# One-layer streaming encoder on one core: tokens, per-layer inputs and cached keys arrive features first, and the gate splits its per-layer inputs itself

## The chip, the core and the metric

The kernel runs on one core of one Trainium2 chip. Times are device microseconds of one execution of the program. The engines of the core are named as in the profile: PE (TensorE matmuls, with its weight loads as PEld), DVE (VectorE), ACT (ScalarE), POOL (GpSimd) and SP (SyncE, which here issues every DMA). The work is fp32 throughout; there is no change of data types between the two kernels.

## The reference

One layer over 2048 prompt tokens and 32 sample tokens, model width 1024, feed-forward width 4096, per-layer input width 256:

```
qa, ka, va, qb, kb, vb = split_proj(rmsnorm(h, g_attn), w_in)     # w_in 1024 x 3072
oa = diff_attn(qa, ka, va, t5_table, lam)     # 4 heads, two 64-wide maps, 128-wide values, chunk-causal
ob = band_attn(qb, kb, vb, band_table)        # 8 heads of 64, own chunk of 64 and the 8 before
h  = h + concat(rmsnorm(oa, subln_g) * (1 - lam_init), rmsnorm(ob, out_norm_b)) @ w_out
h  = h + relu(rmsnorm(h, g_mlp) @ w_up)**2 @ w_down
h  = h + (p @ w_ple_proj) * sigmoid(h @ w_ple_gate)               # p: per-layer input, 256 wide
y  = rmsnorm(h, g_final)
```

The sample tokens attend to cached keys and values (128 past rows) as well. Outputs are y for prompt and samples and the new keys and values of both attention groups.

## The kernel before

**Arithmetic.** A matmul of fp32 accuracy is made of three in a rounded fp32 form (fp32r): each operand is split into a high part (a copy in fp32r, on ACT or DVE) and a low part (operand minus high part, on POOL or DVE), and `mm3` (L213 to L218) adds high by high, low by high and high by low in PSUM. Splits are made by `split` (L178 to L187): ACT's part is L181, POOL's are L166 and L176, DVE's is L187. Weights come from HBM in units of 512 KB through `wunit` (L189): a load into a buffer `wr`, then `wh` (ACT) and `wl` (POOL).

**Layout.** The tokens are cut into four blocks of 512 (the last has the 32 samples too, 544). Activations are held with features on the partitions: `aH` and `aL` are 128 partitions x 8 x 512, eight groups of 128 features. The inputs arrive with tokens as rows, so the kernel turns them on PE, by a matmul against the identity matrix (`ident`).

**Stages**, with their place in the profiled execution, in us:

- 0 to 70: `prep` of blocks 0 and 1, and the value projection of attention group A. `prep` (L360) goes by tiles of 128 tokens: it loads `x` (512 KB), squares it on ACT (the sum for the norm), turns it in eight 128x128 pieces into `xp` in PSUM (L380), makes of each piece `aH` on ACT times the gain `g_attn` (L385) and `aL` on DVE (L386), copies `xp` to `xt` on DVE (L389), and stores `xt` as `xT` (512 KB) for the later residual. The value projection `vtile` (L418) makes 16 groups of 24 matmuls (`vps`): for each of two halves of the value weights and each of eight token tiles. ACT brings a group out of PSUM as `vraw` (L434, a ring of two buffers); from it DVE makes the split `vhl` (also a ring of two), and two stores go out, `va_p` (the output, 128 KB) and `vSa` (256 KB).
- 70 to 187: the bias tables, and the query and key projection of group A for blocks 0 and 1 (`qps`, 512 wide), woven with `prep_p`, which loads the per-layer inputs, turns them (`ppt`, L907), splits them and stores the split as `pS`.
- 187 to 476: attention A for the first queries, woven with group B's projections of blocks 0 and 1 and with `prep` of blocks 2 and 3.
- To about 1000: the projections of blocks 2 and 3, the cached keys and values (`caches`, L536, which turns the cached keys, `ctp`, L546), attention B, and the output projection of blocks 0 and 1.
- 1000 to 2080: the two first MLPs with the rest of attention A between, and the gate of block 1.
- 2080 to the end: output projections, MLPs and gates of the other blocks. `gate` (L1323) loads the split per-layer inputs (`pT`, four loads of 256 KB from `pS`), splits the residual `h` (`hu`), projects both and applies the sigmoid (`sig`).

**What sets the order.** The program is written as generators that are woven step by step; a scheduler at build time then fixes the order of every engine's instructions by readiness and priority (`prep` of blocks 2 and 3 has a raised priority). Each engine works its list in order. All DMAs are issued from SP's list, in order, and each of them waits until the one eight places before it has landed, so that at most eight are in flight. A buffer ring gives a buffer to the next user only when all who read it, stores included, are done.

Of the kernel before, what the change touches and what calls it, by code (L numbers as in the profile page):

```python
# [20 lines left out]
P = 128  # L21
# [122 lines left out]
class Kern:  # L144
# [95 lines left out]
    def consts(self, cp):  # L240
# [13 lines left out]
        self.g_attn = cols("g_attn_s", a["g_attn"][0], 8)  # L254
        self.rcol = cp.tile([P, 17], F32, name="rcol")

    def gains(self, cp):
        nc, a = self.nc, self.a

        def cols(name, ap, k):  # L260
            t = cp.tile([P, k], F32, name=name)
            self.dma(t, ap.rearrange("(k p) -> p k", p=P))
            return t

        self.g_mlp = cols("g_mlp_s", a["g_mlp"][0], 8)
        self.g_b = cols("g_b_s", a["out_norm_b"][0], 4)
        self.g_sub = cols("g_sub_s", a["subln_g"][0], 1)
# [75 lines left out]
    def scratch(self):  # L343
        self.xT = self.dram([P, 8, T], F32, "xT")
# [7 lines left out]
        self.pS = self.dram([P, 2, 2, T], F32, "pS")  # L352
# [7 lines left out]
    def prep(self, b, acts, pp, mm, tag, first=None):  # L360
# [3 lines left out]
        for i, (c0, n) in enumerate(toks(b)):  # L364
            t0 = 512 * b + c0
            x = pp.tile([P, D], F32, tag="x", name="x")
            self.dma(x[:n], self.xsrc(t0, n))
            if first is not None:
                first()
                first = None  # L370
            xt = pp.tile([P, 8, P], F32, tag="xt", name="xt")
            st = pp.tile([P, 1], F32, tag="st", name="st")
            nc.scalar.activation(
                xt[:n].rearrange("p a b -> p (a b)"), x[:n], AF.Square, accum_out=st[:n]
            )
            for h in range(2):
                xp = mm.tile([P, 4, P], F32, tag=tag, name="xp")
                for k in range(4):
                    kk = 4 * h + k
                    nc.tensor.transpose(xp[:, k, :n], x[:n, kk * P : kk * P + P], self.ident[:n, :n])  # L380
                for k in range(4):
                    kk = 4 * h + k
                    g = self.g_attn[:, kk : kk + 1]
                    hi, lo = aH[:, kk, c0 : c0 + n], aL[:, kk, c0 : c0 + n]
                    nc.scalar.activation(hi, xp[:, k, :n], AF.Copy, scale=g)  # L385
                    nc.vector.scalar_tensor_tensor(  # L386
                        lo, xp[:, k, :n], g, hi.bitcast(F32), op0=ALU.mult, op1=ALU.subtract
                    )
                nc.vector.tensor_copy(xt[:, 4 * h : 4 * h + 4, :n], xp[:, :, :n])  # L389
# [500 lines left out]
    def prep_p(self, sg, wk, ps):  # L890
        nc, a = self.nc, self.a
        for b in range(4):
# [4 lines left out]
            if b == 3:  # L897
                self.dma(pn[:SS, 4], a["p_sample"][0, 0])
# [817 lines left out]
```

## Time and profile before

| | |
|---|---|
| median of 3 runs | 3105.26 us (3106.78, 3105.26, 3100.71) |
| profiled execution, its own time | 3106.68 us |
| its span | 3104.9 us |
| PE busy | 2990.2 us, 96% of the span, 17801 matmuls |
| DVE, ACT, POOL busy | 1826.0, 1776.4, 1852.7 us |
| HBM read, written | 421.97 MB, 117.75 MB, 174 GB/s over the span |
| DMA packets under 512 bytes | 38749 of 523279 |

In a row of a view by windows, behind the stretch in us stand its length, then the busy time of PE, PEld, DVE, ACT and POOL with the number of instructions, then the clock that was granted to PE (1.00 is the full one), the mean busy share of the DMA engines, and GB/s. In a row of the timeline stand the start in us, the length, the engine, the line, what is written from what, and how many in a row; in square brackets is the idle time before it and what ended it. In a row of groups the busy time and the mean ns of one stand behind the bar, and then the idle time before such instructions. A tile's row has duration minimum, median and maximum in ns, and the first and last start. Matmuls overlap in their pipeline, so what a matmul adds is read from the distance of two starts.

### The profile page before, as it was taken

The numbers are of one execution on the slowest core, as the hardware profiler recorded it, in microseconds if no ns is written. First come the engines' busy times: TensorE is split into PE (matmuls) and PEld (weight loads), VectorE is DVE, ScalarE is ACT, GpSimd is POOL, SyncE is SP. The second block draws the span as 40 slices with busy tenths as digits, with TensorE's granted clock in tenths as the row PEclk, the third lists the DMA queues.
The fourth block names the chain that finished last, engine by engine and source line by source line (L and its number), as shares of the span: only waits on it lengthen the run. The fifth ranks groups of instructions, "written<-read, shape, count | busy, mean of one in ns | idle before, by whom it ended". The sixth has DMA issues, their size and how long they took to land. (4 is left out here: it accounts for less than half of the span.)

```text
span 3104.9 us, 51763 instructions
## 1 busy us (share of the span) xinstructions
PE 2990.2 (96%) x17801; PEld 2637.0 (85%) x17801; DVE 1826.0 (59%) x4404; ACT 1776.4 (57%) x3434; POOL 1852.7 (60%) x2512
## 2 busy tenths in 40 slices
PE   8999989999899999999999999999899999999998
PEld 7788879899777888878888888878788887999998
DVE  6157565564565455456666656635667885576663
ACT  6256565765666666556556556554655555554545
POOL 2456746413446544556655555677878888767674
PEclk9999999999999999999999999999999999999999
DMA  9798776976877554555655454348434446333231
GB/s 283 258 263 247 224 218 187 280 221 186 247 230 226 159 155 136 154 157 167 196 152 140 124 145 139 123 150 260 155 116 130 146 158 226 118 109 102 90 117 57
DMA packets 523279, 539.19 MB, mean 174 GB/s; under 512 B 38749, under 2 KB 401569, under 8 KB 523017
## 3 DMA queue, kind: packets, MB, share of 16 engines
q1 hardware_dynamic: 523016, 535.89, 57.5%
q8 instruction: 141, 2.31, 0.3%
q14 instruction: 122, 0.99, 0.1%
HBM read 421.97 MB, written 117.75 MB: 174 GB/s over the span
## 5 line engine op out<-in xcount | busy, mean ns | idle before, releaser
L176 POOL TENSOR_TENSOR wl<-wr,wh 128x256 fp32r<-128x256 f32 x648 | 478.9, 771 | 317.8 <-ACT wh L181 277.9
L181 ACT ACTIVATE piece<-wr 128x512 fp32r<-128x512 f32 x406 | 245.4, 624 | 265.0 <-PE ups L217 111.2
L176 POOL TENSOR_TENSOR piece<-wr,piece 128x256 fp32r<-128x256 f32 x404 | 327.5, 836 | 104.6 <-ACT piece L181 85.7
L181 ACT ACTIVATE wh<-wr 128x1024 fp32r<-128x1024 f32 x228 | 240.4, 1055 | 188.1 <-PE ups L217 46.8
L166 POOL TENSOR_TENSOR wl<-wr,wh 128x256 fp32r<-128x256 f32 x264 | 201.9, 797 | 188.1 <-ACT wh L181 185.3
L216 PE MATMUL dps<-uh,piece 128*128 128x272 f32 (+1 forms) x768 | 246.3, 324 | 6.2 <-DVE h L1217 2.5
L166 POOL TENSOR_TENSOR piece<-wr,piece 128x256 fp32r<-128x256 f32 x280 | 235.1, 871 | 26.7 <-ACT piece L181 25.5
L218 PE MATMUL dps<-uh,piece 128*128 128x272 f32 (+1 forms) x768 | 246.9, 324 | 1.8 <-POOL piece L166 1.6
L217 PE MATMUL dps<-ul,piece 128*128 128x272 f32 (+1 forms) x768 | 247.3, 323 | 0.2 <-DVE ul L187 0.2
L216 PE MATMUL ups<-cs,piece 128*128 128x256 f32 (+1 forms) x864 | 245.8, 285 | 0.9 <-DVE r L1228 0.8
L217 PE MATMUL ups<-cs,piece 128*128 128x256 f32 (+1 forms) x864 | 245.7, 285 | 0.0
L218 PE MATMUL ups<-cs,piece 128*128 128x256 f32 (+1 forms) x864 | 245.5, 284 | 0.0
L216 PE MATMUL qps<-aH,wh 128*128 128x512 f32 (+1 forms) x640 | 227.9, 357 | 1.1 <-DVE ql L488 1.1
L217 PE MATMUL qps<-aL,wh 128*128 128x512 f32 (+1 forms) x640 | 228.0, 356 | 0.0
L218 PE MATMUL qps<-aH,wl 128*128 128x512 f32 (+1 forms) x640 | 227.6, 356 | 0.0
L1217 DVE TENSOR_TENSOR h<-h,dps 128x272 f32<-128x272 f32 (+1 forms) x384 | 188.9, 514 | 52.6 <-PE dps L218 51.7
L1169 DVE TENSOR_TENSOR h<-h,dps 128x512 f32<-128x512 f32 x256 | 173.3, 682 | 69.0 <-PE dps L218 67.4
L665 ACT ACTIVATE e<-e,nm 128x128 f32<-128x128 f32 (+16 forms) x136 | 157.2, 1156 | 94.9 <-DVE nm L663 92.9
L216 PE MATMUL dps<-uh,wh 128*128 128x512 f32 x512 | 207.0, 404 | 1.8 <-DVE h L1169 1.8
L216 PE MATMUL ups<-cH,wh 128*128 128x512 f32 x512 | 202.8, 397 | 1.9 <-ACT cH L181 1.9
L217 PE MATMUL ups<-cL,wh 128*128 128x512 f32 x512 | 202.5, 396 | 1.8 <-POOL cL L166 1.2
L218 PE MATMUL ups<-cH,wl 128*128 128x512 f32 x512 | 202.7, 396 | 0.0
(311 smaller groups left out, 9369.8 us busy)
## 6 DMA issues: line engine op xcount, KB each, us to landing
wr<-w_up SPq DMA_DIRECT2D x128, 512.0 KB, 4.0
wr<-w_down SPq DMA_DIRECT2D x128, 512.0 KB, 3.9
wr<-w_in SPq DMA_DIRECT2D x74, 512.0 KB, 5.5
q<-qS SPq DMA_DIRECT2D x128, 256.0 KB, 5.2
v<-vSa SPq DMA_DIRECT2D x64, 512.0 KB, 4.8
ka<-kS SPq DMA_DIRECT2D x32, 512.0 KB, 6.8
wr<-w_out SPq DMA_DIRECT2D x32, 512.0 KB, 4.6
wr<-w_ple_gate SPq DMA_DIRECT2D x32, 512.0 KB, 4.2
```

Source lines behind the costliest of these rows:

```text
L166: nc.gpsimd.tensor_tensor(out[:, sl], a[:, sl], b[:, sl], op=op)
L176: nc.gpsimd.tensor_tensor(out[:, sl], a[:, sl], b[:, sl], op=op)
L181: nc.scalar.activation(hi, raw, AF.Copy)
L216: nc.tensor.matmul(ps, lh, rh, start=start and i == 0, stop=False)
L217: nc.tensor.matmul(ps, lh, rl, start=False, stop=False)
L218: nc.tensor.matmul(ps, ll, rh, start=False, stop=stop and i == n - 1)
L665: nc.scalar.activation(row, row, AF.Exp, bias=nmx, accum_out=z[:nr, m : m + 1])
L1169: nc.vector.tensor_tensor(hv, hv, ps, op=ALU.add)
L1217: nc.vector.tensor_tensor(hv, hv, ps, op=ALU.add)
```

## The change

The host hands over three arrays that it has laid out with numpy: `x_t` (128 x 8 x 2080, the tokens with features first), `p_t` (128 x 2 x 2080, the per-layer inputs likewise) and `ck_t` (the cached keys of both groups, features first). The four gain vectors come as [128, k], so that a partition's values lie together.

`prep` loads, for each tile of 128 tokens, the tile of `x_t` (`xt`) and the rows `x`; DVE multiplies `xt` by the gain in place, ACT and DVE split it, and ACT squares `x` in place for the sum. Nothing is turned and `xT` is not stored, since `x_t` takes its place. `prep_p` and `pS` are gone; the query and key projection of group A is no longer woven with anything. A new function `ptile` loads two raw halves of the per-layer inputs (`praw`) for a gate and splits them there; block 0's is called ahead of the output projection of block 2. `caches` loads the cached keys features first. The value weights' raw loads of the first stage have four buffers of their own (`wr0`) beside the ring `wr`.

```diff
     def wunit(self, src, shape, hi_eng="act", lo_eng="pool", pool=None):
         nc = self.nc
-        raw = self.rawp.tile([P] + shape, F32, bufs=2, name="wr")
+        if pool is None:
+            raw = self.rawp.tile([P] + shape, F32, bufs=2, name="wr")
+        else:
+            raw = pool.tile([P] + shape, F32, tag="wr0", bufs=4, name="wr0")
...
-            self.dma(t, ap.rearrange("(k p) -> p k", p=P))
+            self.dma(t, ap)
...
-        self.xT = self.dram([P, 8, T], F32, "xT")
+        self.xT = self.a["x_t"]
+        self.pT = self.a["p_t"]
...
-            x = pp.tile([P, D], F32, tag="x", name="x")
-            self.dma(x[:n], self.xsrc(t0, n))
+            xt = pp.tile([P, 8, P], F32, tag="xt", name="xt")
+            self.dma(xt[:, :, :n], self.xT[:, :, t0 : t0 + n])
...
-            xt = pp.tile([P, 8, P], F32, tag="xt", name="xt")
+            x = pp.tile([P, D], F32, tag="x", name="x")
+            self.dma(x[:n], self.xsrc(t0, n))
+            m = 2 if b == 0 and i == 0 else 1
+            for k in range(0, 8, 8 // m):
+                ks = slice(k, k + 8 // m)
+                xg = xt[:, ks, :n]
+                g = self.g_attn[:, ks].unsqueeze(2).broadcast_to([P, 8 // m, n])
+                nc.vector.tensor_tensor(xg, xg, g, op=ALU.mult)
+                self.split(aH[:, ks, c0 : c0 + n], aL[:, ks, c0 : c0 + n], xg, "act", "dve")
             st = pp.tile([P, 1], F32, tag="st", name="st")
-            nc.scalar.activation(
-                xt[:n].rearrange("p a b -> p (a b)"), x[:n], AF.Square, accum_out=st[:n]
-            )
-            for h in range(2):
-                xp = mm.tile([P, 4, P], F32, tag=tag, name="xp")
-                for k in range(4):
-                    kk = 4 * h + k
-                    nc.tensor.transpose(xp[:, k, :n], x[:n, kk * P : kk * P + P], self.ident[:n, :n])
-                for k in range(4):
-                    kk = 4 * h + k
-                    g = self.g_attn[:, kk : kk + 1]
-                    hi, lo = aH[:, kk, c0 : c0 + n], aL[:, kk, c0 : c0 + n]
-                    nc.scalar.activation(hi, xp[:, k, :n], AF.Copy, scale=g)
-                    nc.vector.scalar_tensor_tensor(
-                        lo, xp[:, k, :n], g, hi.bitcast(F32), op0=ALU.mult, op1=ALU.subtract
-                    )
-                nc.vector.tensor_copy(xt[:, 4 * h : 4 * h + 4, :n], xp[:, :, :n])
-            self.dma(self.xT[:, :, t0 : t0 + n], xt[:, :, :n])
+            nc.scalar.activation(x[:n], x[:n], AF.Square, accum_out=st[:n])
...
-            kn = sg.tile([P, 512], F32, tag="kn", bufs=2, name="ckn")
-            self.dma(kn, ck)
-            tps = tp.tile([P, 4, P], F32, tag="mm", name="ctp")
-            for g in range(4):
-                nc.tensor.transpose(tps[:, g], kn[:, P * g : P * g + P], self.ident)
+            tf = sg.tile([P, BLK], F32, tag="kr", bufs=2, name="ckr")[:, :512]
+            self.dma(tf, ck)
...
-    def prep_p(self, sg, wk, ps):
...
+    def ptile(self, b, up, wk):
+        n, t0 = BN[b], 512 * b
+        pT = [[up.tile([P, BLK], F32R, tag="u", name="pT") for _ in range(2)] for _ in range(2)]
+        for k in range(2):
+            raw = (
+                up.tile([P, up.aw], F32, tag="u", name="praw") if wk is None
+                else wk.tile([P, BLK], F32, tag="tmp", bufs=self.nt, name="praw")
+            )[:, :n]
+            self.dma(raw, self.pT[:, k, t0 : t0 + n])
+            self.split(pT[0][k][:, :n], pT[1][k][:, :n], raw, "act", "dve")
+        return pT
+
-        for i in range(2):
-            for k in range(2):
-                self.dma(pT[i][k][:, :n], self.pS[:, i, k, t0 : t0 + n])
+        if pT is None:
+            pT = self.ptile(b, up, wk)
...
-                qk = self.proj(HALVES[0], 0, acts, sg, mm, Rings((ps_t, "tp")), vs=())
-                weave(qk, self.prep_p(sg, wk, ps_t), 2)
+                drain(self.proj(HALVES[0], 0, acts, sg, mm, Rings((ps_t, "tp")), vs=()))
...
+                pT = self.ptile(0, up, wk)
                 weave(self.outproj(2, wk, oa[2], md, acc[2]), self.oload(3, wk, act, oa), 1, 0, 2)
...
-            g = self.gate(0, h, up, None, md, wk, made[0])
+            g = self.gate(0, h, up, None, md, wk, made[0], pT)
```

Where the instructions then stand is fixed by the scheduler. SP's list in the first stage, around the first store of values (`va_p`), before; `wr` with 4x256 are value weights, with 8x128 query and key weights, and x_4486 is a tile of block 2:

```order
L157 DMA x_423<-x_prompt 128x1024
L157 DMA wr_1188<-w_in 128x8x128
L157 DMA wr_1380<-w_in 128x8x128
L157 DMA x_4486<-x_prompt 128x1024
L157 DMA wr_227<-w_in 128x4x256
L157 DMA x_536<-x_prompt 128x1024
L157 DMA wr_236<-w_in 128x4x256
L157 DMA xT_83<-xt_125 1024x1x128
L157 DMA va_p<-vraw_277 128x256
L157 DMA x_643<-x_prompt 128x1024
L157 DMA vSa_86<-vhl_279 128x512
L157 DMA xT_83<-xt_186 1024x1x128
```

And now, on the same engine, at the same store; ahead of these rows stand eight loads of xt and x for block 0 and four of value weights, and xt_4182 and x_4184 are block 2's first tile:

```order
L157 DMA wr_901<-w_in 128x8x128
L157 DMA wr_976<-w_in 128x8x128
L157 DMA wr_1061<-w_in 128x8x128
L157 DMA wr_1144<-w_in 128x8x128
L157 DMA xt_4182<-x_t 128x8x128
L157 DMA x_4184<-x_prompt 128x1024
L157 DMA x_439<-x_prompt 128x1024
L157 DMA xt_437<-x_t 128x8x128
L157 DMA va_p<-vraw_228 128x256
L157 DMA vSa_85<-vhl_230 128x512
L157 DMA x_521<-x_prompt 128x1024
L157 DMA xt_519<-x_t 128x8x128
```

The first store of values stood behind 13 transfers of 512 KB and now stands behind 20, of which four are query and key weights and two belong to block 2.

ACT's list in the first stage, where blocks 0 and 1 meet, before; `aH_107<-xp` are single 128x128 pieces of block 1:

```order
L385 ACTIVATE aH_107<-xp_541,g_attn_s_122 128x128
L434 ACTIVATE vraw_309<-vps_284,rcol_124 128x256
L434 ACTIVATE vraw_384<-vps_359,rcol_124 128x256
L373 ACTIVATE xt_538,st_539<-x_536 128x1024
L385 ACTIVATE aH_107<-xp_555,g_attn_s_122 128x128
L385 ACTIVATE aH_107<-xp_541,g_attn_s_122 128x128
```

And now; vraw_310 is the third use of the ring of two, so it follows the store `va_p<-vraw_228` above, aH_105 is block 1's, and rsv and rsy are steps of a tile's norm:

```order
L181 ACTIVATE wh_1063<-wr_1061 128x1024
L396 ACTIVATE rbt_107<-rp_431 128x512
L384 ACTIVATE x_4184,st_4189<-x_4184 128x1024
L226 ACTIVATE rsv_4191<-st_4189 128x1
L228 ACTIVATE rsy_4193<-rsv_4191 128x1
L384 ACTIVATE x_439,st_444<-x_439 128x1024
L229 ACTIVATE rsy_4193<-rsy_4193 128x1
L226 ACTIVATE rsv_446<-st_444 128x1
L228 ACTIVATE rsy_448<-rsv_446 128x1
L229 ACTIVATE rsy_448<-rsy_448 128x1
L428 ACTIVATE vraw_310<-vps_285,rcol_122 128x256
L181 ACTIVATE aH_105<-xt_437 128x8x128
```

ACT's many small pieces became one instruction per tile, and squares of later tiles, block 2's among them, stand ahead of the third `vraw`.

ACT's list at the gate of block 2, before; `hu` is the split of the residual, `piece` that of weights, `uh` that of the MLP's hidden layer, `sig` the first step of the sigmoid:

```order
L181 ACTIVATE uh<-r_29347 128x512
L181 ACTIVATE piece<-wr 128x512 x2
L181 ACTIVATE hu<-h 128x512
L181 ACTIVATE piece<-wr 128x512 x2
L181 ACTIVATE hu<-h 128x512 x7
L181 ACTIVATE piece<-wr 128x512 x3
L1362 ACTIVATE sig<-gps 128x512
```

And now:

```order
L181 ACTIVATE uh<-r_28816 128x512
L181 ACTIVATE piece<-wr 128x512 x2
L181 ACTIVATE pT<-praw 128x512 x2
L181 ACTIVATE hu<-h 128x512 x2
L181 ACTIVATE piece<-wr 128x512 x2
L181 ACTIVATE hu<-h 128x512 x6
L181 ACTIVATE piece<-wr 128x512 x5
L1334 ACTIVATE sig<-gps 128x512
```

The two splits of the per-layer inputs stand ahead of the first split of the residual.

More of the change, by code (lines that the diff above doesn't have):

```diff
@@ L1687, with columns @@
 }
+def columns(*parts):
+    t = np.concatenate(parts).T
+    return np.ascontiguousarray(t.reshape(-1, P, T).transpose(1, 0, 2))
 def kernel(**inputs):
     arrays = {k: np.ascontiguousarray(v) for k, v in inputs.items()}
-    for n in ("cache_a_k", "cache_a_v", "cache_b_k", "cache_b_v"):
+    for n in ("cache_a_v", "cache_b_v"):
         arrays[n] = arrays[n].reshape(PAST, 512)
+    ck = [arrays.pop(n).reshape(PAST, 4, P) for n in ("cache_a_k", "cache_b_k")]
+    arrays["ck_t"] = np.ascontiguousarray(np.stack(ck).transpose(0, 3, 2, 1)).reshape(2, P, 512)
+    arrays["x_t"] = columns(arrays["x_prompt"][0], arrays["x_sample"][0])
+    arrays["p_t"] = columns(arrays.pop("p_prompt")[0, 0], arrays.pop("p_sample")[0, 0])
+    for n in ("g_attn", "g_mlp", "out_norm_b", "subln_g"):
+        arrays[n] = np.ascontiguousarray(arrays[n].reshape(-1, P).T)
     arrays["onehot_a"], arrays["onehot_b"] = onehots()
```

43 lines of the change are left out of this document (7 added, 36 removed).

## The prediction

> **What bounds the kernel now.** I read the page's busy shares first, then the windows by stage, and then the rows of each tile that the change touches.
>
> ```profile
> PE 2990.2 (96%) x17801; PEld 2637.0 (85%) x17801; DVE 1826.0 (59%) x4404; ACT 1776.4 (57%) x3434; POOL 1852.7 (60%) x2512
> ```
> ```profile
> 0.00:25.00 25.00, 16.07 (x93) 14.27 (x94) 13.33 (x47) 17.82 (x52) 8.58 (x19) 1.00 0.94 277
> 25.00:50.00 25.00, 23.86 (x201) 23.26 (x201) 19.98 (x67) 21.59 (x65) 11.92 (x18) 1.00 1.07 334
> 50.00:70.00 20.00, 20.00 (x170) 19.91 (x169) 9.89 (x35) 6.77 (x19) 0.00 (x0) 1.00 0.67 225
> 70.00:187.00 117.00, 114.21 (x567) 91.66 (x566) 27.29 (x69) 33.38 (x60) 45.62 (x66) 1.00 0.82 257
> 187.00:476.00 289.00, 268.75 (x1591) 235.40 (x1590) 184.61 (x550) 179.25 (x413) 185.44 (x270) 0.97 0.80 235
> ```
>
> PE is busy 96% of the span, so work taken from PE shortens the program unless PE then waits. The exception is the first 50 us: the DMA share is 0.94 and 1.07 there, at 277 and then 334 GB/s. From 70 to 187 us PE idles 2.8 us in 117, and from 187 to 476 20 us in 289. There the granted clock also falls, to 0.97, after long gaps:
>
> ```profile
> 326.67 0.58 PE L723 MATMUL o<-pH,v 128*128 128x256 f32 x1 [3.39 <-ACT rsv L223]
> 398.68 1.01 PE L650 MATMUL s<-ka,q 128*128 128x384 f32 x2 [4.87 <-DVE e L657]
> ```
> ```profile
> 327.00:336.00 9.00, 9.00 (x38) 7.97 (x38) 3.70 (x9) 4.20 (x10) 6.78 (x10) 0.69 0.85 260
> ```
> ```profile
> 399.00:407.00 8.00, 8.00 (x46) 7.91 (x46) 6.60 (x21) 5.55 (x14) 3.74 (x5) 0.67 0.60 187
> ```
>
> A gap of 3.39 us is followed by 9 us at 0.69, which loses 9 x 0.31 = 2.8 us more, and one of 4.87 us by 8 us at 0.67, 2.6 us more. I price a gap above about 3 us at its length plus 2.7.
>
> **The price of a turn on PE.** The 136 `xp` and 34 `ppt` transposes and the 8 `ctp` go.
>
> ```profile
> L380 PE MATMUL xp<-ident,x 128*128 128x128 f32 (+1 forms) x136 | 21.5, 289 | 6.2 <-DMA x<-x_prompt 4.4 <-DVE kr L493 1.1 <-ACT vraw L434 0.5
> ```
> ```profile
> 391.80 0.60 PE L380 MATMUL xp<-ident,x 128*128 128x128 f32 x4
> 392.24 0.82 PE L709 MATMUL tpp<-ident,e 128*128 128x128 f32 x6
> ```
>
> Four of them push the next instruction back by 392.24 - 391.80 = 0.44 us, 0.11 each; the whole group is busy 21.5 us, 0.158 each. I take 0.12, near the start-to-start value, since the busy time counts overlap with neighbours.
>
> **First stage, 0 to 70 us: +5.9 us.** 64 of the `xp` are here, 64 x 0.12 = 7.7 us of PE. If PE alone set its end, that would be the gain. But the stores decide:
>
> ```profile
> L218 PE MATMUL vps<-wh,aL x128: 277/283/582, 10.1 to 69.3; 128*128 128x256 f32 x128
> ```
> ```profile
> 36.37 1.83 PE L380 MATMUL xp<-ident,x 128*128 128x128 f32 x12
> 39.20 0.39 PE L216 MATMUL vps<-wh,aH 128*128 128x256 f32 x1 [1.00 <-ACT vraw L434]
> 39.43 0.28 PE L217 MATMUL vps<-wl,aH 128*128 128x256 f32 x1
> 39.55 0.28 PE L218 MATMUL vps<-wh,aL 128*128 128x256 f32 x1
> ```
> ```profile
> 17.98 3.04 SPq L157 DMA_DIRECT2D va_p<-vraw  x1
> ```
>
> The 16 `vps` groups end at 69.3 + 0.3 = 69.6. A matmul of them follows the one before by 39.55 - 39.43 = 0.12 us; over a long stretch 0.117, so a group of 24 takes 2.81. A group can start only when one of three PSUM banks is free, and ACT frees a bank by writing `vraw`, a ring of two that waits for the store `va_p`. Already before, PE stood 1.00 us for that at 39.20. The first `va_p` was issued at 17.98, behind 13 transfers of 0.524 MB. In SP's new order it stands behind 20, 10.5 MB. The first 25 us moved 25 x 0.277 = 6.9 MB. So it lands at about 25 + (10.5 - 6.9) / 0.334 = 36 us, and until then ACT stands at the third `vraw`, with the splits of block 1's tiles queued behind it. The store that frees the 8th group's bank is the third `va_p`, with 16.0 MB of transfers ahead of it by the same count: 25 + (16.0 - 6.9) / 0.334 = 52.2 us. The other bound takes the best rate of a stretch that I found, some 410 GB/s from 2584 to 2591 us (this row has 40 slices of 1 us from 2580 on):
>
> ```profile
> GB/s 335 349 383 409 409 406 417 415 400 413 417 347 324 352 385 403 337 332 362 409 414 409 404 349 306 291 305 356 383 377 376 338 236 100 291 176 8 237 287 44
> ```
>
> At 0.41 it is 25 + 9.1 / 0.41 = 47.2. From there nine groups take 9 x 2.81 = 25.3 us, so the stage ends between 72.5 and 77.5, plus 0 to 2.7 for a half clock after one gap. I take 75.5, the middle, +5.9 against 69.6; the ends are -7.7 (stores in time) and +13.3 (below). DVE and ACT have less to do: a tile costs DVE 8 x 0.343 + 2 x 0.678 = 4.1 us now and 2 x 1.382 = 2.8 at most then, and ACT 8 x 0.365 = 2.9 now and 1.06 then, by these rows (the three-operand one stands for an fp32 pass of 128x1024 on DVE):
>
> ```profile
> L386 DVE SCALAR_TENSOR_TENSOR aL<-xp,g_attn_s,aH 128x128 fp32r<-128x128 f32 x128 | 42.3, 343 | 29.4 <-ACT aH L385 29.2
> L389 DVE COPY xt<-xp 128x512 f32<-128x512 f32 x32 | 21.7, 678 | 0.0
> L671 DVE SCALAR_TENSOR_TENSOR e<-e,c 128x1024 f32<-128x1024 f32 x40 | 55.1, 1382 | 8.1 <-ACT e L670 8.1
> ```
> ```profile
> L385 ACT ACTIVATE aH<-xp,g_attn_s 128x128 fp32r<-128x128 f32 (+1 forms) x136 | 45.8, 365 | 23.5 <-DVE aL L386 21.1 <-PE xp L380 1.7 <-PE qps L217 0.3
> L181 ACT ACTIVATE wh<-wr 128x1024 fp32r<-128x1024 f32 x228 | 240.4, 1055 | 188.1 <-PE ups L217 46.8 <-issue 32.1 <-PE qps L217 20.8
> ```
>
> The gains as [128, k] spare SP a stand of at most 2.00 us, the one at `g_b_s`; the first group waits for weights and splits anyway, so nothing (0 to -2):
>
> ```profile
> 4.79 2.00 SPq L157 DMA_DIRECT2D g_b_s<-out_norm_b  x1
> ```
>
> **Query and key stage, 70 to 187 us: -6.2 us.** The 34 `ppt` go, 34 x 0.12 = 4.1 us, and with them two PE waits in the ring of PSUM banks that `ppt` shares with `ktp`, 1.82 + 0.33 = 2.1:
>
> ```profile
> 105.22 0.66 PE L516 MATMUL ktp<-ident,kr 128*128 128x128 f32 x4 [1.82 <-ACT kn L518]
> 106.44 0.66 PE L907 MATMUL ppt<-ident,pn 128*128 128x128 f32 x4 [0.33 <-DVE ppl L911]
> ```
>
> The stage is PE-bound (114.21 of 117), so what goes comes out: bounds -4 and -8.
>
> **Blocks 2 and 3, 187 to 476 us: -8.6 - 1.6 - 2.0 us.** 72 `xp` go: 72 x 0.12 = 8.6 (7.9 to 11.4), and PE's waits before them, 1.1 for `kr` and 0.5 for `vraw` in the group's row above. The rest of the gaps belong to attention's chain through DVE and ACT. These two lose work, 72 x 0.365 = 26 us on ACT and 9 tiles x 1.3 = 12 us on DVE, but the scheduler has redrawn the order of this whole stretch. I give -2, with -8 (a third of the 20 us of gaps closes) and +10 (three more gaps of the kind priced above) as the ends. **Cached keys**: 8 transposes, -1.0.
>
> **The gates: +4.0 us.** ACT splits the per-layer inputs twice per gate (0.63 us each) ahead of the residual's first split, and is in order: `hu` and the sigmoid's steps queue behind it, POOL's low parts wait for ACT, and PE for these. At the gate of block 2:
>
> ```profile
> 2597.60 0.63 ACT L181 ACTIVATE hu<-h 128x512 fp32r<-128x512 f32 x1 [1.11 <-DVE h L1217]
> 2599.85 1.15 ACT L181 ACTIVATE piece<-wr 128x512 fp32r<-128x512 f32 x2 [1.62 <-DMA wr<-w_ple_gate]
> 2600.91 3.55 ACT L181 ACTIVATE hu<-h 128x512 fp32r<-128x512 f32 x6
> ```
> ```profile
> 2590.44 0.38 SPq L157 DMA_DIRECT2D wr<-w_ple_gate  x1
> 2601.52 5.01 SPq L157 DMA_DIRECT2D pT<-pS  x4
> ```
> ```profile
> cs<-cSt SPq DMA_DIRECT2D x8, 544.0 KB, 10.1
> ```
>
> `pT` was fetched at 2601.52, after `hu` had begun. Now `praw` must be there before 2597.60. It is issued about where the weights of 2590.44 are, behind transfers that take 10.1 us to land, so about 2601: 3.4 late, and two splits of 0.63 make 4.7. ACT idled 1.62 us there for the weights, which hides that much: +3 (0 to +7.7, the whole 5 plus 2.7 for a half clock). Gates 1 and 3 get 0.5 each, between nothing and 2 x 0.63. At block 0's gate, where `ptile` comes early, ACT has room, so 0:
>
> ```profile
> 2062.73 1.06 ACT L181 ACTIVATE wh<-wr 128x1024 fp32r<-128x1024 f32 x1 [4.24 <-PE gps L217]
> ```
>
> **The sum.** +5.9 - 6.2 - 8.6 - 1.6 - 2.0 - 1.0 + 4.0 = -9.5, from the span of 3104.9 to 3095.4. The profiled execution took 3106.68, 1.8 above its span, and the median of the runs is 1.4 below it; 3106.7 - 9.5 - 1.4 = 3096 us.
>
> **Rivals.** *The stores land in time*, 3082: SP's prefetch costs nothing and the first stage gives its 7.7 us too (13.6 less than my sum). For it: DVE and ACT are lighter there. Against it: PE already waited for `vraw` with seven transfers fewer ahead. *The first stage is set by DMA*, 3103: the 8th group starts at 52.2 and two gaps above 3 us come before it, 52.2 + 25.3 + 5.4 = 82.9, 13.3 over 69.6 and 7.4 over my sum. For it: the DMA share of 1.07. *Slower, 3115*: ACT stands at the first `praw` split. If that costs gates 1, 2 and 3 the whole of 5 + 2.7 = 7.7 us each, it is 23.1 instead of 4.0. It decides for slower once these stands exceed 4.0 + 15.5 = 19.5 us together. For it: at 2597.60 PE has nothing but this gate to do. Against it: ACT's idle time at gates 1 and 3.
>
> The Trainium skill, in "TensorE: Matmul & The Clock Gate", Part 1, has the clock halve after an idle window of about 3.4 us and come back after about 3.4 us of steady work. By that a gap costs an estimated 1.7 us beyond itself, and the second rival would come to 3101; the trace's 9 us at 0.69 after a gap of 3.39 speak for more, and I keep the measured price.
>
> **How the numbers follow.** My forecast, with its own range of 3085 to 3104, has a chance of 0.46; stores in time 0.15; DMA-set first stage 0.16; slower by the gates 0.23. A measurement of this kernel tells about 0.2%, 6.2 us, from no change: 3099 to 3111.5 is "the same". Of the forecast's 0.46, 0.10 lies above 3099. So faster is 0.36 + 0.15 = 0.51, the same 0.10 + 0.16 = 0.26, slower 0.23. The range is 3079 to 3116: it takes in the rivals' times, and leaves 2 in 10 for sums of ends on one side.
>
> **What would show it.** In the profile after: the last `vps` near 75 us, with PE gaps ended by `vraw` between 25 and 55 and `vraw` ended by `va_p`; if the last comes before 65, the first rival. The query and key stage about 6 us shorter, and no gap at `ktp`. From 187 to the end of attention A's first part, 8 to 12 us less. At the gates, ACT's splits of `praw` with the load as releaser: where these waits pass 5 us, the last rival. I am wrong if the redrawn stretch costs more than its +10, or if later stages, whose PE order is unchanged, move.

## The result, and the profile after

The changed kernel takes 3075.25 us (median of 4 runs, 3073.95 to 3077.8) against 3102.99 us for the kernel before beside it: a ratio of 0.991, 95% interval 0.9894 to 0.9926, some 28 us faster. A second set of runs gave 0.9927 (0.9905 to 0.9948). Forecast were 3096 us and a range of 3079 to 3116, so the direction was right and the size was not.

The page's busy times after, and the windows after, cut at four places that both programs pass: the last value matmul of the first stage, the first score of attention A, the first score of attention B, and the first matmul of the first MLP.

```profile
PE 2965.4 (96%) x17623; PEld 2617.9 (85%) x17623; DVE 1815.5 (59%) x4268; ACT 1760.9 (57%) x3314; POOL 1870.7 (61%) x2512
```
```profile
0.00:78.60 78.60, 56.63 (x393) 54.20 (x394) 44.99 (x106) 43.63 (x99) 27.24 (x36) 0.93 0.96 302
78.60:175.70 97.10, 96.05 (x424) 75.27 (x423) 16.67 (x40) 27.23 (x51) 40.98 (x59) 1.00 0.75 234
175.70:528.80 353.10, 346.63 (x2242) 313.25 (x2239) 209.86 (x556) 206.02 (x404) 255.98 (x353) 1.00 0.78 229
528.80:952.10 423.30, 399.58 (x2438) 353.75 (x2439) 240.23 (x809) 281.71 (x595) 165.91 (x260) 0.97 0.79 230
952.10:1989.00 1036.90, 1019.82 (x5222) 858.44 (x5220) 609.89 (x1572) 627.18 (x1055) 577.71 (x818) 1.00 0.53 152
1989.00:3074.70 1085.70, 1046.72 (x6913) 962.93 (x6912) 693.83 (x1189) 575.12 (x1114) 802.84 (x989) 0.99 0.42 137
```

The same cut of the kernel before, in its windows:

```profile
0.00:69.60 69.60, 59.53 (x457) 57.12 (x458) 42.92 (x145) 46.01 (x134) 20.50 (x35) 1.00 0.91 282
69.60:177.90 108.30, 105.55 (x495) 82.90 (x493) 21.90 (x41) 28.41 (x46) 45.58 (x66) 1.00 0.79 255
177.90:547.50 369.60, 346.85 (x2181) 309.88 (x2181) 222.28 (x656) 221.04 (x494) 231.69 (x337) 0.98 0.77 228
547.50:981.20 433.70, 410.89 (x2554) 366.91 (x2555) 239.34 (x815) 286.35 (x607) 173.77 (x271) 0.98 0.80 231
```

A stage's length less PE's busy time is PE's idle time there. The first stage grew by 9.0 us. The query and key stage shrank by 11.2. From the first score to the first MLP 803.3 us became 776.4, 26.9 less; 15.4 of it is idle time (22.8 + 22.8 before, 6.5 + 23.7 after), nearly all of it between the first scores of attention A and B. The MLPs with attention A between took 1.2 us more and the rest, with all four gates, 2.3 less (1088.0 before).

### The profile page after: what moved, and what is told of

Same layout as the page of the kernel before. It is cut to its first block, busy times and chain, and to the rows that moved or that the text cites. A ratio compares the mean times of both kernels' runs of the same rounds, so it can differ in the third digit from the quotient of the medians.

```text
span 3074.7 us, 51058 instructions
## 1 busy us (share of the span) xinstructions
PE 2965.4 (96%) x17623; PEld 2617.9 (85%) x17623; DVE 1815.5 (59%) x4268; ACT 1760.9 (57%) x3314; POOL 1870.7 (61%) x2512
## 5 line engine op out<-in xcount | busy, mean ns | idle before, releaser
L176 POOL TENSOR_TENSOR wl<-wr,wh 128x256 fp32r<-128x256 f32 x648 | 493.0, 793 | 276.1 <-ACT wh L181 243.9
L166 POOL TENSOR_TENSOR wl<-wr,wh 128x256 fp32r<-128x256 f32 x264 | 200.2, 790 | 203.2 <-ACT wh L181 185.6
L220 PE MATMUL dps<-ul,wh 128*128 128x512 f32 x512 | 201.8, 394 | 0.0
L221 PE MATMUL dps<-uh,wl 128*128 128x512 f32 x512 | 201.7, 394 | 0.0
```

What stands on the lines that cost most here:

```text
L166: nc.gpsimd.tensor_tensor(out[:, sl], a[:, sl], b[:, sl], op=op)
L176: nc.gpsimd.tensor_tensor(out[:, sl], a[:, sl], b[:, sl], op=op)
L220: nc.tensor.matmul(ps, lh, rl, start=False, stop=False)
L221: nc.tensor.matmul(ps, ll, rh, start=False, stop=stop and i == n - 1)
```

## The experiments

The ratio is always to the kernel before, run beside it (median about 3104 us), and the idle time is PE's between the first scores of attention A and B, from one profile. Two profiles of one program can differ by some us: the changed kernel's second had a span of 3081.3 against 3074.7, and 6.2 us of this lay between first score and first MLP; for the kernel before, this stretch was 6.9 us shorter in the second. So a difference of one profile counts from about 7 us on.

The idle time between the two scores is not all: some orders have less of it there and more behind it. So this table gives the stages in us, with the whole stretch from the first score to the first MLP and PE's idle time in it:

| kernel | first stage | query and key | first score to first MLP | PE idle in that |
|---|---|---|---|---|
| before, two profiles | 69.6, 70.0 | 108.3, 108.3 | 803.3, 796.4 | 45.6, 44.2 |
| changed, two profiles | 78.6, 79.8 | 97.1, 96.6 | 776.4, 782.6 | 30.2, 36.5 |
| token part alone | 84.0 | 114.9 | 771.4 | 32.9 |
| per-layer part alone | 70.0 | 99.3 | 795.7 | 40.7 |
| before, first redraw | 67.5 | 106.7 | 789.5 | 35.2 |
| before, third redraw | 69.4 | 103.6 | 797.0 | 40.7 |
| changed, turns in blocks 2 and 3 | 76.1 | 95.8 | 786.4 | 33.3 |
| changed, all turns | 65.1 | 96.0 | 786.0 | 34.2 |
| changed, all turns and their store | 73.9 | 95.9 | 785.7 | 32.5 |

### The two halves of the change

Token part alone (before, with `x_t`, the new `prep` as in the change, and the four weight buffers):

```diff
-        self.xT = self.dram([P, 8, T], F32, "xT")
+        self.xT = self.a["x_t"]
```

> The kernel before with the token part alone (x_t from the host, the new prep, the four raw weight buffers); per-layer inputs, cached keys and gains as before. If the per-layer part is worth what the prediction counted (query and key stage -6.2, cached keys -1.0, gates +4.0), this is about 3 us slower than the whole change, some 3078 us. If, as the two traces suggest, the gates cost nothing, it is 8 to 9 us slower, some 3084. Both theories of the attention stretch (187 to 476 us before: less small work on ACT and DVE, or the turns gone from PE's order and PSUM banks) expect the stretch's gain of 27 us between the first score and the first MLP to be here whole.

Measured: 1.0009 (0.9994 to 1.0023), no change. The last value matmul comes at 83.7 us, and PE's gap for `vraw` is longer than in the whole change:

```profile
39.15 0.58 PE L219 MATMUL vps<-wh,aH 128*128 128x256 f32 x1 [6.87 <-ACT vraw L428]
```

Per-layer part alone:

```diff
-                qk = self.proj(HALVES[0], 0, acts, sg, mm, Rings((ps_t, "tp")), vs=())
-                weave(qk, self.prep_p(sg, wk, ps_t), 2)
+                drain(self.proj(HALVES[0], 0, acts, sg, mm, Rings((ps_t, "tp")), vs=()))
...
+            pT = self.ptile(b, up, wk)
```

> The kernel before with the per-layer part alone (p_t from the host, no prep_p, the gates split). The prediction's terms: -6.2 in the query and key stage and +4.0 at the gates, some 3101 us. With gates that cost nothing: some 3096 us. A theory by which any redrawing of the order is worth ten or more us either way expects it to lie outside 3090 to 3106.

Measured: 0.9948 (0.9927 to 0.9968), 16 us faster, where the terms of the prediction gave 2. Its idle time is 13.7 us, with all 136 turns still there. The token part, which takes most work from PE, earned nothing alone, so what was expected of its time fell. What was expected of the stretch held: in its profile (3098.68 us, where the median is 3106.12) the stretch from first score to first MLP is 25 to 32 us shorter than before. The first stage, 14 us longer, and the query and key stage, 7 longer, eat most of this.

### Did turns and pieces hold PE up?

Pieces of 128x128 again in blocks 2 and 3, without turns; and turns without a reader, without pieces:

```diff
-                self.split(aH[:, ks, c0 : c0 + n], aL[:, ks, c0 : c0 + n], xg, "act", "dve")
+                for kk in range(8):
+                    self.split(aH[:, kk, c0 : c0 + n], aL[:, kk, c0 : c0 + n], xt[:, kk, :n], "act", "dve")
```

> The changed kernel, with the splits of blocks 2 and 3 made again in eight pieces of 128x128 per tile on ACT and DVE (from SBUF, no turns on PE): per tile ACT 8 x 0.365 = 2.9 us instead of 1.06. Theory W (the attention stretch became shorter since ACT and DVE, in order, have fewer small instructions between attention's steps): PE's gaps in that stretch come back, +12 to +16 us, some 3089. Theory P (it became shorter since the turns are gone from PE's order and from the PSUM banks that the projections use): no change beyond 3 us.

```diff
+                xp = mm.tile([P, 4, P], F32, tag=tag, name="xp")
+                for k in range(4):
+                    kk = 4 * h + k
+                    nc.tensor.transpose(xp[:, k, :n], x[:n, kk * P : kk * P + P], self.ident[:n, :n])
```

> The changed kernel, with the 72 turns of blocks 2 and 3 back on PE, into the same PSUM banks, and nobody reading them (work added that serves nothing). Theory W: PE's work alone, 72 x 0.12 = +8.6 us, some 3084. Theory P: the turns' waits for loads and banks come back too, +18 to +24 us, some 3096.

Measured: 0.9946 (0.9928 to 0.9965) with pieces, 6 to 11 us slower than the changed kernel by its two ratios, and 0.9976 (0.9959 to 0.9994) with turns, 15 to 20 slower. The profiles say less: spans of 3075.9 and 3083.0, idle times of 12.3 and 6.4 us. Neither brings the 22.8 back. But the two profiled executions took 3077.65 and 3084.81 us, where the medians are 3083.27 and 3097.34, so they do not show all that these kernels lose. Whole preparations as before in blocks 2 and 3 settle what the turns do there (`prep_old` is the `prep` of before without its store):

```diff
-lifted(self.prep(2, acts, pp, mm, "mm"))
+lifted(self.prep_old(2, acts, pp, mm, "mm"))
...
-lifted(self.prep(3, acts, pp, mm, "mm"))
+lifted(self.prep_old(3, acts, pp, mm, "mm"))
```

> The changed kernel, with blocks 2 and 3 prepared as before (turns on PE, small pieces on ACT and DVE from PSUM, the copy on DVE; only the store of the turned block stays out), all else changed. Theory T (turns and small pieces, coupled through PSUM, hold PE up in the attention stretch): 72 x 0.12 = 8.6 us and some 14 us of idle time come back, +20 us or more, idle 18 us or more between the first score and attention B. Theory L (the draw of the order did it): +8.6 us, +6 to +12 in all, idle 6 to 12 us.

Measured: 0.992 (0.9902 to 0.9939) beside 0.9927 for the changed kernel in the same set, so no dearer, where 6 us were the least expected, and 7.2 us idle. The windows of this kernel from first score to attention B, and from there to the first MLP:

```profile
171.90:514.20 342.30, 335.12 (x2163) 301.21 (x2161) 224.45 (x656) 220.37 (x494) 231.12 (x332) 1.00 0.76 225
514.20:958.30 444.10, 418.02 (x2614) 375.69 (x2615) 243.39 (x826) 291.42 (x616) 179.09 (x281) 0.97 0.81 232
```

All the turns, small pieces and copies of these blocks are in them, and in the first PE still waits a third of what it did before; over the whole stretch it waits 33.3 us, between the changed kernel's 30.2 and 36.5. So the turns and their small pieces are not what held PE up (theory T falls). Their own price is not refuted: the stretch is 4 to 10 us longer than in the changed kernel's two profiles, for 72 turns put at 8.6, and the first stage 2.5 to 3.7 us shorter. The changed kernel beside it:

> The changed kernel itself, beside the runs of the other kernels of this call, so that they have a common scale: the ratio to the kernel before that it had, 0.991, within its interval of 0.989 to 0.993. If the earlier ratio was an accident of one chip, it lies nearer to 1.

### Was it the order that the scheduler drew?

The kernel before again, and three redraws of it that keep all its work:

> The kernel before itself, for a second profile. If the 22.7 us of PE idle time between its first score and attention B's first (69.6, 177.9 and 547.5 us) belong to its order of instructions, they stand there again, 20 to 25 us, with the gaps of 3.39 and 4.87 us at the same matmuls. If they were an accident of one execution, some 10 us.

```diff
                 nc.vector.tensor_copy(xt[:, 4 * h : 4 * h + 4, :n], xp[:, :, :n])
             self.dma(self.xT[:, :, t0 : t0 + n], xt[:, :, :n])
+            if b > 1:
+                nc.scalar.activation(x[:n], x[:n], AF.Square, accum_out=st[:n])
```

> The kernel before, with all its work; only in blocks 2 and 3 the square for the norm is written behind the turns and in place, so that the scheduler draws the order from 187 us on anew. Theory L (the kernel before had an unlucky order there, 20 us of PE idle time between 178 and 514 us, and any redrawing gets rid of it): that idle time falls to 6 to 11 us and the kernel becomes 8 to 14 us faster than before. Theory T (turns and small pieces themselves hold PE up): still some 20 us idle, within 4 us of before.

```diff
-                weave(qk, self.prep_p(sg, wk, ps_t), 2)
+                drain(qk)
+                drain(self.prep_p(sg, wk, ps_t))
```

> The kernel before, with all its work; only the turning of the per-layer inputs is written behind the query and key projection instead of woven with it. Theory L: the order behind it is drawn anew, and the idle time between 178 and 514 us falls by about 10 us, 8 to 12 us faster than before (some 3092). Theory T: within 4 us of before.

```diff
-                weave(qk, self.prep_p(sg, wk, ps_t), 2)
+                weave(qk, self.prep_p(sg, wk, ps_t), 1)
```

> The kernel before, with the turning of the per-layer inputs woven after every step of the query and key projection instead of every second: no work added or taken, a large redraw. Theory L (the order before was an unlucky one): idle time between first score and attention B of 10 to 14 us, and 6 to 12 us faster than before. If the work that was removed had made the difference: some 20 us idle and within 4 us of before.

The kernel before repeats itself, at 1.0004, with 22.2 us idle and a gap at the same score:

```profile
398.47 1.01 PE L650 MATMUL s<-ka,q 128*128 128x384 f32 x2 [5.99 <-DVE e L657]
```

The three redraws, in the order above: 0.998 (0.9965 to 0.9995) with 10.7 us idle, 1.0012 (0.9997 to 1.0027) with 20.6, and 0.9971 (0.9959 to 0.9983) with 12.8. The window of the second profile of before, and of the last redraw:

```profile
178.30:543.80 365.50, 343.35 (x2181) 308.26 (x2181) 222.12 (x655) 220.84 (x494) 231.69 (x336) 0.98 0.79 230
```
```profile
173.00:519.60 346.60, 333.76 (x2144) 298.97 (x2142) 221.90 (x655) 218.60 (x493) 232.81 (x331) 1.00 0.79 236
```

One figure in a weave, no work taken, and 9 to 10 us of idle time between the two scores and 9 us of the whole time are gone. Over the whole stretch it is less, 40.7 us idle against 45.6 and 44.2, since some of it came back behind attention B's first score. The first redraw has 35.2 there, as little as the changed kernel, and gained 6 us, less than the 8 expected of it; the second, whose stages are cut by other matmuls and so are not in the table, has 46.1 and gained nothing. The whole stretch of the first redraw:

```profile
174.20:526.80 352.60, 341.85 (x2165) 305.66 (x2166) 220.15 (x660) 219.31 (x496) 228.60 (x332) 0.99 0.80 236
526.80:963.70 436.90, 412.45 (x2571) 368.75 (x2570) 238.63 (x813) 286.27 (x605) 172.15 (x269) 0.98 0.79 230
```

So a draw alone can close most of these gaps, not every draw does, and it moves this kernel by up to 9 us. It is the same on the other side, with the same kind of edit on the changed kernel:

```diff
-lifted(self.prep(2, acts, pp, mm, "mm")), 3)
+lifted(self.prep(2, acts, pp, mm, "mm")), 2)
```

> The changed kernel, with block 2's preparation woven after every second step of the projection instead of every third: no work added or taken, a small redraw of the order. Theory L: idle time between first score and attention B stays 6 to 12 us, the time within 6 us of the changed kernel. If the changed kernel's order was the lucky one, it is 6 to 14 us slower.

Measured: 0.9941 (0.9922 to 0.9959), 4 to 10 us slower than the changed kernel by its two ratios, with 10.0 us idle, as the changed kernel's second profile has too (10.1).

### The first stage

Rings of four for `vraw` and `vhl` in that stage:

```diff
-        raw = sg.tile([P, 256], F32, tag="vraw", bufs=2, name="vraw")
+        raw = (vp or sg).tile([P, 256], F32, tag="vraw", bufs=4 if vp else 2, name="vraw")
```

> The changed kernel, with the buffers of the value stage (vraw and vhl) in rings of four in that stage instead of two. The prediction's step (a store of values behind 20 transfers holds ACT, and with it PE's banks): the 4.35 us gap at 32.9 us goes, the last value matmul comes at 66 to 72 us instead of 78.4, and the kernel is 6 to 12 us faster than the changed one, some 3067. If the loads themselves set the stage's end, it stays within 2 us.

The changed kernel's own weight buffers taken out, and then the rings of four with the first `x` behind the weights:

```diff
-        if pool is None:
-            raw = self.rawp.tile([P] + shape, F32, bufs=2, name="wr")
-        else:
-            raw = pool.tile([P] + shape, F32, tag="wr0", bufs=4, name="wr0")
+        raw = self.rawp.tile([P] + shape, F32, bufs=2, name="wr")
```

> The changed kernel without the four raw weight buffers of its own (value weights go through the shared ring again, so that query and key weights compete with them). The prediction's step counts only the bytes ahead of the stores: about as many, so within 4 us of the changed kernel. If the early landing of the value weights was what those buffers give, the first groups start later and it is 5 or more us slower.

```diff
+            if b == 0 and i == 0:
+                yield
+            x = pp.tile([P, D], F32, tag="x", name="x")
+            self.dma(x[:n], self.xsrc(t0, n))
             st = pp.tile([P, 1], F32, tag="st", name="st")
```

> The changed kernel with rings of four in the value stage, and the first tile's rows x loaded behind the first value weights. The first matmul waited for its weights (11.0 us with the rings of four); it now starts 1.5 to 2.5 us earlier, the stage ends some 2 us earlier, 62 us. Some 12 to 16 us faster than the changed kernel. If the stores set it, it ends at 64 as with the rings alone.

The rings gave 0.9867 (0.9845 to 0.9889), 3068 us, more than expected, and the last value matmul at 64.2 instead of 78.4:

```profile
L221 PE MATMUL vps<-wh,aL x128: 277/283/420, 12.2 to 64.2; 128*128 128x256 f32 x128
```

Only one gap for `vraw` above 0.8 us is left, of 0.81. With the shared weight ring the kernel was at 0.991 as before: those buffers are worth nothing measurable. With the first rows `x` behind the weights the first matmul starts at 8.5 us, the stage ends at 62.2, and the time is 3062.84 us (0.9873, 0.9857 to 0.989). It beats both kernels, by some 17 us the changed one in the same set; against the rings alone the two ratios agree within their intervals.

### What the token part is worth

Four kernels put turns back into the changed one: in blocks 0 and 1; in all blocks; in all blocks with the store of the turned tokens; and in all blocks, without the store, with the rings of four as above.

```diff
-gen = (y for b in HALVES[0] for y in self.prep(b, acts, pp, ring, "s", first if b == 0 else None))
+gen = (y for b in HALVES[0] for y in self.prep_old(b, acts, pp, ring, "s", first if b == 0 else None))
...
+            self.dma(self.xT[:, :, t0 : t0 + n], xt[:, :, :n])
```

> The changed kernel, with blocks 0 and 1 prepared as before (tokens as rows alone, 4.2 MB fewer loads in the first stage, 64 turns on PE), all else changed. The prediction's first stage (stores behind too many loads cost more than the turns): the first value store now stands behind 16 transfers instead of 20, the last value matmul comes at 66 to 71 us instead of 78.4, and the kernel is 5 to 12 us faster than the changed one, turns and all. If PE's work set the stage, the 64 turns would make it 7 us slower.

> The changed kernel with blocks 0 to 3 all prepared as before (136 turns, small pieces, copies; no store of the turned tokens); per-layer inputs, cached keys, gains and weight buffers as changed. If token part and per-layer part simply add (0.9 us slower and 0.5% faster, alone), it stands where the per-layer part alone did: some 3086 us. If the token part earns nothing beside the other, it stands at the changed kernel's time or below, since its first stage ends earlier: 3070 to 3080.

> The change without its token part: blocks prepared wholly as before, the store of the turned tokens included, x_t not handed over; per-layer inputs, cached keys, gains and weight buffers as changed. If the rest of the change makes all of the gain, about the time of all turns put back without the store (3068, ratio 0.989), at most 3 us more for 17 stores of 512 KB. If handing over x_t earns by sparing these stores in the first stage, where DMA is full, some 3078: its stage ends at 70 us or later instead of 65.

> All turns put back without the store, with the rings of four in the value stage. With turns the stage had no wait for vraw left, so by the reading of the gaps the rings give nothing: within 4 us of 3068. If the stores still held it there, it ends 3 us earlier or more, some 3063.

Turns in blocks 0 and 1 alone gave 0.9911 (0.9892 to 0.993), against 0.9927 beside it, no difference clear of noise, with the last value matmul at 71.1 us. Turns in all four blocks, with the store of the turned tokens left out because the residual reads `x_t`, gave 0.9889 (0.9874 to 0.9904), 3067.8 us: faster than the changed kernel by both its ratios, and than both expectations, with 136 turns more on PE. With that store back, so that nothing of the token part is left but the weight buffers, it was 0.9935 (0.9918 to 0.9952). The last value matmul with all turns, without and with the store:

```profile
L221 PE MATMUL vps<-wh,aL x128: 276/282/581, 9.2 to 64.8; 128*128 128x256 f32 x128
```
```profile
L221 PE MATMUL vps<-wh,aL x128: 277/283/579, 9.9 to 73.6; 128*128 128x256 f32 x128
```

What DMA moved in the first 65 us, in the same order, and in the changed kernel:

```profile
DMA packets 15943, 16.36 MB, mean 252 GB/s; under 512 B 1936, under 2 KB 12976, under 8 KB 15937
```
```profile
DMA packets 22885, 18.67 MB, mean 287 GB/s; under 512 B 1754, under 2 KB 20570, under 8 KB 22879
```
```profile
DMA packets 23842, 20.10 MB, mean 309 GB/s; under 512 B 1821, under 2 KB 21277, under 8 KB 23837
```

Among these three the stage ends in the order of the bytes: 65.1, 73.9, 78.6 us. The bytes alone do not set it, though. The kernel before, and the changed kernel with rings of four, moved as much as the second of these and ended at 69.6 and 64.5:

```profile
DMA packets 24940, 18.96 MB, mean 292 GB/s; under 512 B 3558, under 2 KB 22502, under 8 KB 24934
```
```profile
DMA packets 20574, 18.84 MB, mean 290 GB/s; under 512 B 2331, under 2 KB 17571, under 8 KB 20568
```

By the ratios `x_t` is worth some 14 us as the residual's source (0.9935 to 0.9889; 8.8 of it is the end of the first stage), and loading the tokens a second time, in `prep`, gives 6 to 12 of them back. Each of these kernels is one draw, and a draw alone moved this kernel by up to 9 us, so the first figure is rough and the second is not clear of the draw. The rings on top of the turns were expected to give nothing; 0.9916 (0.9902 to 0.9929) is 8 us slower, though the stage ends at 63.6. Why is open. Its profile has a new gap in the next stage, which is 8 us longer than without the rings, but this execution took 3067.69 us, as long as without the rings, where the median is 3078.98. So the gap does not explain the 8 us:

```profile
119.34 1.09 PE L557 MATMUL ktp<-ident,kr 128*128 128x128 f32 x4 [6.22 <-ACT qh L181]
```

## Why the prediction was right or wrong

What each term became, in the first profiles of the two kernels and in the second ones (us):

| | forecast | first profiles | second profiles |
|---|---|---|---|
| first stage | +5.9 | +9.0 | +9.8 |
| query and key stage | -6.2 | -11.2 | -11.7 |
| first score to first MLP | -13.2 | -26.9 | -13.8 |
| from the first MLP on, with the gates | +4.0 | -1.1 | -4.4 |
| span | -9.5 | -30.2 | -20.1 |

So the sum was 11 to 21 us too high, and not by one term: the gates make 5 to 8 of it, the query and key stage 5, blocks 2 and 3 between 1 and 14, and the first stage missed the other way.

**What bounds the kernel: right**, with the exception that it named. The 178 turns left PE's list, and PE's busy time fell by 24.8 us.

**First stage, +5.9: right that the stores and their rings hold it, +9.0 in size.** PE's wait for `vraw`, and ACT's third and fifth `vraw` with what stands ahead of each:

```profile
37.25 0.58 PE L219 MATMUL vps<-wh,aH 128*128 128x256 f32 x1 [4.35 <-ACT vraw L428]
```
```profile
36.58 0.20 ACT L229 ACTIVATE rsy<-rsy 128x1 f32<-128x1 f32 x1
36.72 0.47 ACT L428 ACTIVATE vraw<-vps,rcol 128x256 f32<-128x256 f32 x1
...
52.08 0.20 ACT L229 ACTIVATE rsy<-rsy 128x1 f32<-128x1 f32 x1
52.19 0.46 ACT L428 ACTIVATE vraw<-vps,rcol 128x256 f32<-128x256 f32 x1
```

The first store was put at 36 us; it was issued at 29.41, landed 7.3 us later, and the third `vraw` followed at 36.72. The third store, on which the 8th group's bank hangs, was put at 47.2 to 52.2; it was issued at 45.07, landed 7.0 us later, and the fifth `vraw` followed at 52.19, the late end. One detail was wrong: ACT did not stand for these two stores. It worked off squares and norms of later tiles that are ahead in its list, up to the same moment, so the trace alone cannot tell the store from ACT's list. The rings of four can: with them these gaps are gone, though SP's list moved too (the first store goes out at 24.31 there). (The 1.00 us at 39.20 in the kernel before, which the prediction reads as a wait for a store, is such a case too: ACT started that `vraw` at 38.66 straight behind other work.) From the late end the prediction's own count gives 77.5 for the stage. The 8th group started 0.5 us after its `vraw`, and from there PE was busy without a break at the full clock, 26.0 us where nine groups had been put at 25.3:

```profile
52.70 0.39 PE L219 MATMUL vps<-wh,aH 128*128 128x256 f32 x1 [1.70 <-ACT vraw L428]
```
```profile
52.70:78.70 26.00, 26.00 (x218) 25.82 (x219) 11.70 (x41) 10.08 (x27) 0.00 (x0) 1.00 0.78 269
```

So the size was off mainly since I took 75.5, near the middle of 72.5 and 77.5. The clock, for which I had allowed 0 to 2.7 us, fell further ahead of that, without adding to the end:

```profile
37.30:42.00 4.70, 4.63 (x25) 4.40 (x25) 4.67 (x12) 2.71 (x6) 2.29 (x3) 0.65 1.11 341
42.00:46.00 4.00, 0.99 (x4) 0.80 (x5) 3.42 (x7) 2.96 (x7) 0.00 (x0) 0.75 1.14 330
46.00:51.00 5.00, 5.00 (x24) 4.65 (x23) 2.54 (x8) 3.08 (x6) 0.00 (x0) 0.52 1.07 363
```

After the gap of 4.35 us PE worked 4.63 us at 0.65 and, after two more gaps of 1.5, another 5 us at 0.52: 4.63 x 0.35 + 5.0 x 0.48 = 4.0 us lost. Behind it PE stood 1.70 us for `vraw` all the same, at 52.70, so the loss was time in which it would have waited. By the Trainium skill ("TensorE: Matmul & The Clock Gate", Part 1), which has the clock at half until about 3.4 us of steady work are done, a gap costs an estimated 1.7 us beyond itself. The 4.0 us measured here, behind a long gap and two short ones, are more. And the stage's loss is the token part's own: it ends at 84.0 us with this part alone, and at 70.0 with the per-layer part alone.

**Query and key stage, -6.2: measured -11.2**, though its end, the first score, is no fixed point of the work: besides the 34 `ppt`, 37 matmuls fewer lie in it, most of which now come in the next stretch. At 0.12 us each these are 4.4 us, about the excess. Over both stages, forecast -0.3, measured -2.2.

**Blocks 2 and 3 and the cached keys, -13.2: measured -26.9 in the first profiles and -13.8 in the second.** The price of the turns fits: with the 72 turns back the stretch took 786.4 and 786.0 us, against 776.4 and 782.6 without them. The step that failed is the redrawn order, "I give -2, with -8 ... and +10": PE's idle time between the first scores fell by 16.3 us in the first profiles and by 12.0 in the second, and over the whole stretch by 15.4 and 7.7, where I had given 3.6. The sentence on which it rests, that the rest of the gaps belong to attention's chain and at most a third might close, took the gaps for a property of the work. A redraw that takes nothing away closes 9 to 10 us of them over the whole stretch, and with all the turns put back they stay closed, at 5.8 and 7.2 between the scores. How much of the gain is the luck of the new order and how much the work that left ACT, DVE and PE with the rest of the change was not isolated: the redraws of the kernel before lie at 35 to 46 us of idle time in the stretch, the changed kernel and its variants in the table at 30 to 37.

**The gates, +4.0: no cost was seen.** From the first MLP on, the changed kernel took 1 to 4 us less than before. At block 2's gate ACT's wait that I forecast is there, 2.70 us where I had put the load 3.4 late:

```profile
2569.24 1.32 ACT L181 ACTIVATE pT<-praw 128x512 fp32r<-128x512 f32 x2 [2.70 <-DMA praw<-p_t]
```

But the PE rows at the same time show no stand:

```profile
2572.18 0.40 PE L221 MATMUL dps<-uh,piece 128*128 128x512 f32 x1
2572.42 0.39 PE L219 MATMUL gps<-hu,piece 128*128 128x512 f32 x1
2572.64 0.39 PE L219 MATMUL pps<-pT,piece 128*128 128x512 f32 x1
2572.88 0.39 PE L220 MATMUL pps<-pT,piece 128*128 128x512 f32 x1
```

PE was busy with the MLP's last matmuls (`dps`) until 2572.4, 3 us after the split had begun, and then the early per-layer inputs gave it `pps` to do while `hu` was split. Before, they were loaded from 2601.52 on, after `hu`, and PE stood 1.83 us for `hu`; now it stood 0.64. The two rows, before and now:

```profile
2606.22 0.51 PE L217 MATMUL gps<-hu,piece 128*128 128x512 f32 x1 [1.83 <-POOL hu L166]
```
```profile
2579.22 0.50 PE L220 MATMUL gps<-hu,piece 128*128 128x512 f32 x1 [0.64 <-POOL hu L166]
```

This step failed too: the +3 put on this gate counted ACT's delay as PE's, without asking how long PE still had work and what the earlier operand let it do. The last rival had the same fault: at 2597.60, where it has PE with nothing but this gate to do, the kernel before still worked on `dps`.

**Rivals.** Stores in time: not so. A first stage set by DMA: in part. Its start of the 8th group at 52.2 came, its 5.4 us for two gaps above 3 us did not, and the 78.6 lies between my 75.5 and its 82.9. Slower by the gates: no. The case that came, an order with 8 to 15 us less idle time and gates that cost nothing, stood in no rival.

## What to carry to other kernels

Where a scheduler draws the order, idle time on the bounding engine may belong to that one draw: redraw the kernel before without taking work away, and see what a draw is worth, before a gain or a loss of a per cent is put down to the change. Loads that are added ahead of the stores that free buffers can cost more than the matmuls they save: here the first stage grew by 9 us with 64 turns fewer, and two more buffers in two rings took 14 us off it. A wait on a side engine is a cost only from the moment the bounding engine runs dry, and an operand that comes early can give it work.

## What was not expected of the hardware

The same program's profiles differ by 6.6 us of span, 6.2 of them in one stretch with many small dependent steps, while the MLP stretch agrees within 0.2 us. And the clock came down to 0.52 over 5 us of unbroken PE work after gaps of only 1.56 and 1.52 us, which followed a gap of 4.35 us with 4.7 us of work between. In the same stage a gap of 1.38 us (before 29.10) and one of 1.70 us (before 52.70) were followed by the full clock. Whether the gap before them makes the difference was not tested.
